# The first column tiles of an MLP's up projection by plain products on the mixer's own hi/lo parts, with the row squares read back from DRAM

## Chip, cores and metric

The kernel runs on one core of one Trainium2 chip. The metric is the device time of one execution in microseconds (us); shorter is better. All tensors are fp32. TensorE (PE) multiplies fp32 by splitting each operand into a high part and a low part and adding three passes (high by high, high by low, low by high), so one logical product costs three matmuls.

## The reference, cut to what matters

One decoder step for 512 prompt rows and 8 sample rows: a pooling mixer, an MLP, an attention layer, a second MLP. The change touches the end of the mixer and both MLPs.

```python
def _rmsnorm(x, g):
    y = x * lax.rsqrt(jnp.mean(x * x, axis=-1, keepdims=True) + RMS_EPS)
    return y * g
def _mlp_block(x, g, w_up, w_down):
    h = jnp.square(jax.nn.relu(_rmsnorm(x, g) @ w_up))
    return x + h @ w_down
# layer 0: x = x + pool_mix(rmsnorm(x, norm_mix[0])); x = _mlp_block(x, norm_mlp[0], ...)
# layer 1: x = x + attention(rmsnorm(x, ...)) @ w_o;  x = _mlp_block(x, norm_mlp[1], ...)
```

D_MODEL is 1024, D_FF 4096. Since relu and the square let a positive factor per row through, the kernel leaves out 1/rms(x) ahead of the up projection and multiplies the down projection's sum by its square, `rstd2`, near the end. So the squares of x are not needed when an MLP begins, only before its seventh block of columns is added up.

## The kernel before

**Layout.** The residual stream lies transposed in SBUF as `xT`: eight tiles (k = 0 to 7) of 128 features by 520 tokens, each token row cut in two halves of 260 (`HN`). A "product" (`product`, L186) is four k-tiles by three passes, 12 matmuls of 128x128 weights by 260 columns into half a PSUM bank. The tags `mm` and `aux` have four banks each.

**The up projection.** FF is cut into eight blocks `c` of 512 columns, each block into two pairs (`i` = 0, 1) of 128-column tiles. One pair is a 2 by 2 by 2 block product (two halves of k, two column tiles, two halves of tokens), which `up` computes by a Strassen-Winograd scheme: seven products instead of eight. For that it needs sums of weights (`fast_w`: VectorE makes four sums `wsum`, ScalarE and VectorE split seven operands into `whi` and `wlo`) and sums of inputs (`fast_x`: t1 to t4, made once per MLP from the scaled x, each split on ScalarE, L288, and VectorE, L289, into tiles named `first`, `xh` and `xl`). `fast_x` cannot begin before the rows of x that it reads are final. The relu output is squared and split (`squared`, L640 to L642) into `hh` and `hl`.

**The down projection.** `down(c)` makes 16 products per block and adds them into `xT` in place (for c = 0 it overwrites it; x itself was stored to a DRAM copy `xd` before and comes back as `xr` while c = 6 is added). Each block runs `up(c, 0)` and `up(c, 1)` interleaved with `down(c-1)` by a string of u and d; in every fifth place a `Steps` generator issues a piece of other work (compression of cached rows, with gathers `gat` on the GpSimd queue and their copies `perm`), after it has skipped its first eight calls.

**Squares.** `add_square` squares a tile of xT on ScalarE (L220, L223) and adds it on GpSimd (POOL, L225) into `sqacc`, through two buffers `sq`. The first MLP does this within its first two pairs; for the second MLP it is done in the loop that applies `w_o`, one square for each tile of xT. `mean_tok` and `spread` turn the sum into `rstd2` once the first pair of c = 1 is done.

**The mixer.** L161 multiplies eight k-tiles of pooled differences (`dh`, `dl`) by the mixer's weights and L604 adds the outcome to xT, on VectorE. Next to it four GpSimd operations (L556, L557, L608, L609) make the normalised rows `us` and `junk` that are stored as outputs, and the page numbers `idx` are made for the gathers.

**Order.** The program is not issued in the order in which it is written: a scheduler places the instructions of each engine by its own timeline, with the written order as priority. Each engine then works through its list strictly in order, and so a wait holds everything behind it. Weight loads (`wraw`, three buffers of 1 MB) go through SP's queue.

Of the kernel before, what the change touches and what calls it, by code (L numbers as in the profile page):

```python
# [9 lines left out]
F32 = mybir.dt.float32  # L10
# [8 lines left out]
P = 128  # L19
D = 1024  # L20
KT = D // P
# [81 lines left out]
def tile_step(ctx, tc, I, O):  # L103
# [6 lines left out]
    def pool(name, bufs=1, **kw):  # L110
        return tc.tile_pool(name=name, bufs=bufs, reuse_waits="tile", **kw)
# [162 lines left out]
    def fast_x(gcol, tp, first):  # L274
# [37 lines left out]
            split("t4", j, t4)  # L312
        return {n: [[t[:, k] for k in range(HK)] for t in hl] for n, hl in xs.items()}

    def part(tp):
        return tp.tile([P, 264], F32, name="part", tag="part", bufs=5)[:, :HN]

# [180 lines left out]
                self.skip = 0  # L498
                self()

    with pool("st") as st:
# [40 lines left out]
        for n, tiles in ((P, (0, 1)), (P, (2, 3)), (NB, (4,))):  # L542
            for i in tiles:
                t = xt[i] if i < 4 else xs
                junk = st.tile([P, D], F32, name="junk", tag="junk", bufs=2)
                S.activation(junk[:n], t, AF.Square, accum_out=ss[:n, i : i + 1])
            c = slice(tiles[0], tiles[-1] + 1)
            V.tensor_scalar(ss[:n, c], ss[:n, c], 1.0 / D, EPS, OP.mult, OP.add)
            rsqrt(rst[:n, c], ss[:n, c], rtmp[:n, c])
            for i in tiles:  # L550
                if i < 4:
                    bi = st.tile([P, 4, 144], F32, name=f"band{i}")
                    V.tensor_scalar(bi, band[:, min(i, 1)], rst[:, i : i + 1], None, OP.mult)
                    bands.append(bi)
                else:
                    G.tensor_scalar(us[:NB], xs, rst[:NB, 4:5], 1.0, OP.mult, OP.mult)  # L556
                    G.tensor_tensor(us[:NB], us[:NB], gbc[:NB], OP.mult)  # L557

        psx = bank()
        for k in range(KT):  # L560
# [11 lines left out]
                V.tensor_copy(dst, b.rearrange("p (k c) -> p k c", k=4))  # L572


        dh = st.tile([P, KT, TOK], F32R, name="dh")
        dl = st.tile([P, KT, TOK], F32R, name="dl")
# [31 lines left out]
        G.tensor_scalar(u3[96:128], xt[3][96:128], rst[96:128, 3:4], 1.0, OP.mult, OP.mult)  # L608
        G.tensor_tensor(u3[96:128], u3[96:128], gbc[96:128], OP.mult)  # L609
        nc.gpsimd.dma_start(O["pool_prompt"].rearrange("b a j d -> (b a j) d"), u3[113:128, :])  # L610
        nc.gpsimd.dma_start(O["pool_sample"][:, 0, 14, :], us[:NB])
        later.append(lambda: nc.sync.dma_start(O["pool_sample"][:, 0, 0:14, :], I["state_pool"][:, 0, 1:15, :]))
# [8 lines left out]
            V.tensor_tensor(idx[:, c], idf[:, c], pgf[:, 1:17], OP.add)  # L621


    def mlp(layer, gcol, mp, first, sqacc=None, filler=None, finish=None):


        xd = dram.tile([P, KT, TOK], F32, name=f"xd{layer}")
# [4 lines left out]
        steps = Steps(filler(mp) if filler else None, 8)  # L632
        nc_ = FF // (HK * P)
        hs = {}

# [9 lines left out]
        def up(c, i):  # L645
# [46 lines left out]
            for p in (p1, p5, p2, p6, p7, p3, p4) if c else (p1, p5, p6, p2, p7, p3, p4):  # L692
                p()
                yield

        def down(c):

            h = [[t[q] for t in hs[c]] for q in range(2)]
            for m in range(KT):
# [5 lines left out]
                for n in range(2):  # L705
# [6 lines left out]
                        V.tensor_tensor(y[:, hn], o, y[:, hn], OP.add)  # L712
                    if n and c == nc_ - 2:
                        x = mp.tile([P, TOK], F32, name="xr", tag="sq", bufs=2)
                        nc.scalar.dma_start(x, xd[:, m])
                        V.tensor_tensor(y, y, rstd2, OP.mult)  # L716
                        G.tensor_tensor(y, y, x, OP.add)  # L717
                    if c == nc_ - 1:
# [5 lines left out]
                            add_square(mp, sqacc, m)  # L724
                    yield

        w0 = fast_w(load_w(lambda r: [(r, wu[0])]), mp)
        xs = fast_x(gcol, mp, first)

        us_ = [up(0, i) for i in range(2)]  # L730
        for n, s_ in enumerate("00101001010111"):
            next(us_[int(s_)])
            if n == 3 and sqacc is None:
                sqacc = [mp.tile([P, TOK], F32, name="sqacc", tag="rs", bufs=1)]
                for k in range(KT):
                    add_square(mp, sqacc, k)
        for c in range(1, nc_):
            d = down(c - 1)
            for i in range(2):
                u = up(c, i)  # L740
# [4 lines left out]
                if c == 1 and i == 0:  # L745
# [20 lines left out]
        )  # L766
    with pool("mlp0") as mp:
        first = [[mp.tile([P, HK, HN], F32R, name=f"first{i}{j}") for j in range(2)] for i in range(3)]
        mean1 = mlp(0, gT[:, 16:24], mp, first, filler=compress_samples)


    with ExitStack() as at_:
# [490 lines left out]
        op_ = mp  # L1263
        sqacc = [op_.tile([P, TOK], F32, name="sqacc", tag="rs", bufs=1)]
# [78 lines left out]
    mlp(1, gT[:, 24:32], mp, first, sqacc, finish=finish)  # L1343
    mlp_.close()
    kx_.close()

# [36 lines left out]
```

## Time and profile before

| | before |
|---|---|
| median of 3 runs | 1203.05 us (1200.61 to 1206.67) |
| profiled execution | 1198.37 us, its span 1196.0 us |
| mean granted PE clock | 0.979 of full speed |
| PE busy | 1138.9 us, 95% of the span |
| DVE / ACT / POOL busy | 881.4 (74%) / 605.3 (51%) / 273.8 (23%) us |

The profile counts an engine busy while an instruction runs; PE's matmuls overlap, so its count of matmuls in a stretch says more than its busy time. The span is what the profiler sees between the first and the last instruction; the 2.4 us beside it are start and end. PE waits little over the whole span, but unevenly: of 40 equal slices the first three are its weakest.

### The profile page before, as it was taken

How to read it: one execution, taken by the hardware profiler on the slowest of the kernel's cores; microseconds unless marked ns; L12 is line 12 of the kernel's file. 1: busy time of each engine (PE TensorE's matmuls, PEld its weight loads, DVE VectorE, ACT ScalarE, POOL GpSimd, SP SyncE). 2: the span in 40 equal slices, each digit the busy share in tenths (PEclk: the TensorE clock that was granted, in tenths of full speed). 3: DMA queues.
4: the chain of work that ended last, by engine and by line, in shares of the span. 5: the costliest groups of instructions: out<-in, count | busy, mean ns of one | idle time of the engine just before them, and what ended most of it. 6: DMA issues, size and time to landing. Idle time of an engine off the chain costs nothing.

```text
span 1196.0 us, 22945 instructions
## 1 busy us (share of the span) xinstructions
PE 1138.9 (95%) x8971; PEld 1061.2 (89%) x8971; DVE 881.4 (74%) x2064; ACT 605.3 (51%) x1340; POOL 273.8 (23%) x311
## 2 busy tenths in 40 slices
PE   5769999999999999999998999999999999999996
PEld 4759999999999989999975665799999999999996
DVE  6888667777767887477678786769866686776885
ACT  4546544454444444554455555745654443544455
POOL 4350000011001323351458643712000000000032
PEclk9769999999999999999999999999999999999998
DMA  9424432343233426353321311143323323233221
GB/s 262 159 79 159 159 106 89 115 126 105 89 115 120 146 80 219 115 148 95 90 53 54 125 54 54 36 129 120 107 89 106 107 73 119 93 104 108 90 71 72
DMA packets 93539, 129.84 MB, mean 109 GB/s; under 512 B 5848, under 2 KB 68944, under 8 KB 92527
## 3 DMA queue, kind: packets, MB, share of 16 engines
q1 hardware_dynamic: 85687, 109.81, 29.4%
q0 software_dynamic: 5120, 14.23, 3.9%
q10 hardware_dynamic: 2624, 4.34, 1.3%
q8 instruction: 70, 1.15, 0.4%
q14 instruction: 38, 0.31, 0.1%
HBM read 115.76 MB, written 17.24 MB: 111 GB/s over the span
## 4 chain that ended last, share of the span: by engine, by line
PE 86%; DVE 6%; DMA 3%; ACT 2%; issue 1%; POOL 1%; SPq 0%; DVEq 0%; ACTq 0%; POOLq 0%
PE aux L191 29%; PE mm L191 27%; PE mm L161 14%; PE aux L1177 3%; PE aux L1204 3%; PE mm L1130 2%; PE aux L405 2%; DMA wraw<-in_w_up_dram 1%; DVE s L1135 1%; DMA wraw<-in_pool_w_dram 1%; POOL sqacc L225 1%; PE aux L236 1%; PE aux L449 1%; DVE wlo L149 1%; DVE wlo L183 1%
## 5 line engine op out<-in xcount | busy, mean ns | idle before, releaser
L191 PE MATMUL aux<-hh,whi 128*128 128x260 f32 x960 | 269.6, 283 | 1.5 <-DVE xT L712 1.5
L191 PE MATMUL aux<-hl,whi 128*128 128x260 f32 x960 | 269.6, 283 | 1.3 <-DVE hl L642 1.3
L191 PE MATMUL aux<-hh,wlo 128*128 128x260 f32 x960 | 266.3, 282 | 0.0
L182 ACT ACTIVATE whi<-wraw 128x512 fp32r<-128x512 f32 x224 | 132.3, 624 | 200.5 <-PE mm L191 155.0
L183 DVE TENSOR_TENSOR wlo<-wraw,whi 128x512 fp32r<-128x512 f32 x224 | 151.7, 701 | 56.1 <-ACT whi L182 51.5
L191 PEld LDWEIGHTS aux<-hl,whi 128*128 128x128 f32 x960 | 180.8, 188 | 1.9 <-DVE hl L642 1.5
L191 PEld LDWEIGHTS aux<-hh,whi 128*128 128x128 f32 x960 | 180.1, 188 | 2.7 <-DVE xT L712 1.2
L191 PEld LDWEIGHTS aux<-hh,wlo 128*128 128x128 f32 x960 | 179.0, 188 | 0.1
L191 PE MATMUL mm<-first,whi 128*128 128x260 f32 x768 | 152.1, 291 | 13.3 <-DVE first L289 8.7
L191 PE MATMUL mm<-xh,wlo 128*128 128x260 f32 x496 | 140.7, 285 | 0.0
L191 PE MATMUL mm<-xl,whi 128*128 128x260 f32 x496 | 140.6, 284 | 0.0
L191 PE MATMUL mm<-xh,whi 128*128 128x260 f32 x496 | 140.5, 284 | 0.0
L191 PEld LDWEIGHTS mm<-first,whi 128*128 128x128 f32 x768 | 124.3, 195 | 15.8 <-DVE first L289 10.2
L712 DVE TENSOR_TENSOR xT<-aux,xT 128x260 f32<-128x260 f32 x192 | 81.5, 424 | 49.0 <-PE aux L191 48.6
L191 PE MATMUL mm<-first,wlo 128*128 128x260 f32 x384 | 111.5, 291 | 3.7 <-DVE wlo L183 3.7
L717 POOL TENSOR_TENSOR xT<-xT,xr 128x520 f32<-128x520 f32 x16 | 24.7, 1546 | 371.1 <-DVE xT L716 371.1
L161 PE MATMUL mm<-xh,whi 128*128 128x260 f32 (+1 forms) x464 | 101.3, 287 | 1.4 <-DVE csm L1141 1.0
L161 PE MATMUL mm<-xl,whi 128*128 128x260 f32 (+1 forms) x464 | 101.9, 287 | 0.0
L161 PE MATMUL mm<-xh,wlo 128*128 128x260 f32 (+1 forms) x464 | 100.9, 286 | 0.0
L183 DVE TENSOR_TENSOR wlo<-wsum,whi 128x512 fp32r<-128x512 f32 x128 | 86.6, 688 | 16.2 <-ACT whi L182 15.6
L182 ACT ACTIVATE whi<-wsum 128x512 fp32r<-128x512 f32 x128 | 77.1, 623 | 38.0 <-PE mm L191 30.3
L191 PEld LDWEIGHTS mm<-xl,whi 128*128 128x128 f32 x496 | 94.1, 190 | 0.4
(329 smaller groups left out, 2527.3 us busy)
## 6 DMA issues: line engine op xcount, KB each, us to landing
wraw<-in_w_up_dram SPq DMA_DIRECT2D x32, 1024.0 KB, 5.9
wraw<-in_w_down_dram SPq DMA_DIRECT2D x32, 1024.0 KB, 5.2
wraw<-in_w_kv_dram SPq DMA_DIRECT2D x6, 1024.0 KB
xd<-xT SPq DMA_DIRECT2D x4, 1040.0 KB, 4.4
xr<-xd ACTq DMA_DIRECT2D x16, 260.0 KB, 3.6
w<-in_cmp_w_dram POOLq DMA_DIRECT2D x32, 128.0 KB, 3.2
wraw<-in_w_qg_dram SPq DMA_DIRECT2D x8, 512.0 KB, 5.6
wraw<-in_w_o_dram SPq DMA_DIRECT2D x16, 256.0 KB, 5.4
```

What stands on the lines that cost most here:

```text
L149: (eng or V).tensor_tensor(l_, raw_ap, f(h_), OP.subtract)
L161: T.matmul(o[n][:m, :HN], w[:, kt, :m], x[:, n * HN : (n + 1) * HN], start=(i == 0 and pi == 0), stop=(i == len(kts) - 1 and pi == 2),)
L182: S.activation(hi, raw_ap, AF.Copy)
L183: V.tensor_tensor(lo, raw_ap, f(hi), OP.subtract)
L191: T.matmul(o, w_[:, kt], x_[kt][:, xs], start=(start and kt == 0 and pi == 0), stop=(kt == HK - 1 and pi == 2), skip_group_check=True,)
L225: G.tensor_tensor(sqacc[0], sqacc[0], t, OP.add)
L405: T.matmul(acc[kv], w_[:, kv, b2], o_[:, b2 : b2 + 512], start=(t == 0 and i == 0 and b2 == 0), stop=(t == 7 and i == 2 and b2 == 1),)
L712: V.tensor_tensor(y[:, hn], o, y[:, hn], OP.add)
L717: G.tensor_tensor(y, y, x, OP.add)
L1130: T.matmul(b[:, : k1 - k0], qs[r][:, qt * P : (qt + 1) * P], ks[br][i][:, k0:k1], start=(i == 0), stop=(i == 1),)
L1177: T.matmul(o[par * HD : (par + 1) * HD], lhsT(par), pTs[par], start=start, stop=stop, skip_group_check=True,)
L1204: T.transpose(b[:, r * P : (r + 1) * P], sts[par][r][:, kt * P : (kt + 1) * P], ident)
```

## The change

1. The first MLP's first three pairs, (c, i) = (0,0), (0,1) and (1,0), go through a new `up_plain`: eight products per pair on x's own parts `xht`, `xlt`, with no sums of inputs or weights. These parts are made inside the mixer's loop (L648, L649 of the kernel after), and the weights of the first pair are loaded and split ahead of the mixer's loop.
2. `fast_t` takes the place of `fast_x` in the first MLP: `early()` makes t1 to t3 and an unsplit t4 while the first pairs run, and `last()` splits t4 into the places of b12 once the third pair no longer reads them.
3. In both MLPs the squares are taken from `xd`: a DMA on the GpSimd queue loads a tile into a `sq` buffer, ScalarE squares it in place, POOL adds it. `square` is called twice per pair in c = 1 and 2, and the mean is made in c = 3. The squares in the `w_o` loop go.
4. The `xr` loads move from ScalarE's queue to GpSimd's.
5. The rows `us` and `junk` are made by two VectorE instructions in place of four on GpSimd; `dh` and `dl` get a pool of their own; the filler skips three calls instead of eight.

```diff
+    def fast_t(gcol, tp, xht, xlt, ts):
...
+        def early():
+            for j in range(HK):
+                a, b = [tp.tile([P, TOK], F32, name="sq", tag="sq", bufs=2) for _ in range(2)]
+                for t, k in ((a, j), (b, j + HK)):
+                    S.activation(t, xT[k], AF.Copy, scale=gcol[:, k : k + 1])
+                t1, t2, t3 = [part(tp) for _ in range(3)]
+                t4 = hold[j // 2][:, j % 2 * HN : (j % 2 + 1) * HN]
+                V.tensor_tensor(t1, a[:, HN:], a[:, :HN], OP.subtract)
+                split("t1", j, t1)
+                V.tensor_tensor(t2, b[:, HN:], t1, OP.subtract)
+                split("t2", j, t2)
+                V.tensor_tensor(t3, b[:, HN:], a[:, HN:], OP.subtract)
+                split("t3", j, t3)
+                V.tensor_tensor(t4, b[:, :HN], t2, OP.subtract)
+
+        def last():
+            for j in range(HK):
+                split("t4", j, hold[j // 2][:, j % 2 * HN : (j % 2 + 1) * HN])
...
-                    G.tensor_scalar(us[:NB], xs, rst[:NB, 4:5], 1.0, OP.mult, OP.mult)
-                    G.tensor_tensor(us[:NB], us[:NB], gbc[:NB], OP.mult)
+                    V.scalar_tensor_tensor(us[:NB], xs, rst[:NB, 4:5], gbc[:NB], OP.mult, OP.mult)
...
+        raw0 = load_w(lambda r: [(r, I["w_up"][0][:, :256].rearrange("(k p) m -> p k m", p=P))])
+        plain0 = [split_q(raw0[:, q * HK : (q + 1) * HK, m * P : (m + 1) * P]) for m in range(2) for q in range(2)]
+        xht, xlt = new_x()
...
+                g_ = gT[:, 16 + k : 17 + k]
+                S.activation(xht[:, k], xT[k], AF.Copy, scale=g_)
+                V.scalar_tensor_tensor(xlt[:, k], xT[k], g_, f(xht[:, k]), OP.mult, OP.subtract)
...
+        def up_plain(c, i):
+
+            if c == i == 0:
+                w = plain[0]
+            else:
+                raw = load_w(lambda r: [(r, wu[c * 2 + i])])
+                w = [split_q(raw[:, q * HK : (q + 1) * HK, m * P : (m + 1) * P]) for m in range(2) for q in range(2)]
+            o = [[bank("mm")[:, :HN] for _ in range(2)] for _ in range(2)]
+            for q in range(2):
+                for m in range(2):
+                    for n in range(2):
+                        product(o[m][n], w[m * 2 + q], xs[f"b{q + 1}{n + 1}"], start=q == 0)
...
-                        nc.scalar.dma_start(x, xd[:, m])
+                        nc.gpsimd.dma_start(x, xd[:, m])
...
+        def square(k):
+            t = mp.tile([P, TOK], F32, name="sq", tag="sq", bufs=2)
+            nc.gpsimd.dma_start(t, xd[:, k])
+            if k in (0, KT - 1):
+                a = mp.tile([P, TOK], F32, name="sqacc", tag="rs", bufs=1) if k == 0 else t
+                S.activation(a, t, AF.Square)
+                sqacc.append(a)
+            else:
+                S.activation(t, t, AF.Square)
+                G.tensor_tensor(sqacc[0], sqacc[0], t, OP.add)
...
-                for q, s_ in enumerate("uuududdudududdd"):
+                for q, s_ in enumerate("uuuududdudududdd" if first_one else "uuududdudududdd"):
...
+                    if c < 3 and q in (3, 10):
+                        square((c - 1) * 4 + i * 2 + q // 10)
...
-                add_square(op_, sqacc, m)
```

Behind the last matmuls of the mixer (L161), PE's list before goes on with the products of two Winograd pairs in turn, on `first` tiles that `fast_x` makes:

```order
120 L161 MATMUL mm<-dl,whi 128x260
121 L161 MATMUL mm<-dh,wlo 128x260
122 L191 MATMUL mm<-first_446,whi 128x260
123 L191 MATMUL mm<-first_447,whi 128x260
124 L191 MATMUL mm<-first_446,wlo 128x260
125 L191 MATMUL mm<-first_446,whi 128x260
126 L191 MATMUL mm<-first_448,whi 128x260
127 L191 MATMUL mm<-first_447,whi 128x260
```

At the same place of the kernel after the products read `xh` and `xl`, the parts that the mixer's loop has written:

```order
116 L161 MATMUL mm<-dl,whi 128x260
117 L161 MATMUL mm<-dh,wlo 128x260
118 L191 MATMUL mm<-xh,whi 128x260
119 L191 MATMUL mm<-xl,whi 128x260
120 L191 MATMUL mm<-xh,wlo 128x260
121 L191 MATMUL mm<-xh,whi 128x260
122 L191 MATMUL mm<-xl,whi 128x260
```

What moved: the sums of inputs no longer stand between the mixer and PE's next work.

In the first MLP, POOL's list after holds a chain of loads and adds, where each load but the first three waits for an earlier add (names: `sq` is the loaded tile, `xd_486` the DRAM copy of x, `sqacc` the sum):

```order
24 L810 DMA sq<-xd_486 128x520 [waits DMAHW7_49,DVE_49,Activation_49]
25 L810 DMA sq<-xd_486 128x520 [waits DVE_49,Activation_49]
26 L810 DMA sq<-xd_486 128x520 [waits DMASW4_49,DMASW2_49,Activation_49]
27 L817 ISA
28 L817 TENSOR_TENSOR sqacc<-sqacc,sq 128x520 [waits Activation_49]
29 L810 DMA sq<-xd_486 128x520 [waits DMASW5_49,Pool_49]
30 L817 TENSOR_TENSOR sqacc<-sqacc,sq 128x520 [waits Activation_49]
```

Before, only adds stood there, each behind a square that ScalarE takes of xT itself.

ScalarE's list in the kernel after, at the start of the second MLP's products (`part` are copies of PSUM that the Winograd sums need, `whi` weight parts); the three squares shown are the fifth to seventh of this MLP, the eighth is the row behind them, followed by a `hh` and two `whi`, and the first four stand further up, in the `w_o` loop:

```order
727 L816 ACTIVATE sq<-sq 128x520 [waits DMASW3_49,Pool_49]
728 L698 ACTIVATE part<-mm 128x260 [waits DVE_49,PE_49]
729 L816 ACTIVATE sq<-sq 128x520 [waits DMASW4_49,Pool_49]
730 L182 ACTIVATE whi<-wraw 128x512 [waits PE_49]
731 L182 ACTIVATE whi<-wsum 128x512
732 L698 ACTIVATE part<-mm 128x260 [waits DVE_49,PE_49]
733 L698 ACTIVATE part<-mm 128x260 [waits DVE_49]
734 L182 ACTIVATE whi<-wsum 128x512 [waits PE_49]
735 L182 ACTIVATE whi<-wraw 128x512
736 L698 ACTIVATE part<-mm 128x260 [waits DVE_49,PE_49]
737 L728 ACTIVATE relu<-relu 128x520 [waits DVE_49]
738 L816 ACTIVATE sq<-sq 128x520 [waits DMASW5_49,Pool_49]
```

Before, the last square stands in front of those copies and waits for xT on VectorE and for POOL:

```order
745 L223 ACTIVATE sq<-xT 128x520 [waits DVE_49,Pool_49]
746 L283 ACTIVATE xg<-xT,gT 128x520
747 L182 ACTIVATE whi<-wsum 128x512 [waits PE_49]
748 L182 ACTIVATE whi<-wsum 128x512
749 L288 ACTIVATE xh<-part 128x260 [waits DVE_49]
```

What moved: although `square` is written in c = 1 and 2, the scheduler has put all eight squares of the second MLP at its very start, and four of them now stand among the copies and splits of the first pairs, behind loads from DRAM.

## Rows read from the trace of the kernel before

**Rows 1.** Windows: length, each engine's busy time (instructions), granted PE clock, DMA share, GB/s.

```profile
36.00:48.00 12.00, 11.93 (x99) 11.72 (x99) 7.75 (x18) 3.20 (x6) 0.00 (x0) 1.00 0.22 90
48.00:60.00 12.00, 5.41 (x18) 4.21 (x18) 12.00 (x21) 12.00 (x29) 9.39 (x10) 0.58 0.53 177
60.00:75.00 15.00, 8.38 (x34) 7.11 (x33) 15.00 (x32) 7.18 (x19) 10.15 (x6) 0.54 0.46 157
75.00:85.00 10.00, 6.14 (x32) 5.84 (x33) 6.96 (x17) 3.54 (x10) 6.04 (x2) 0.66 0.00 0
85.00:90.00 5.00, 5.00 (x44) 5.00 (x43) 4.46 (x9) 3.92 (x10) 0.00 (x0) 1.00 0.05 12
900.00:1000.00 100.00, 100.00 (x836) 100.00 (x835) 70.02 (x134) 43.82 (x87) 0.00 (x0) 1.00 0.33 106
```

**Rows 2.** Waits from 48 to 85 us: engine, line, releaser, total, times, longest.

```profile
POOL gat L373 <- PE mm L161: 17.1, 1, 17.1
ACT sq L223 <- POOL sqacc L225: 9.0, 1, 9.0
PE mm L191 <- DVE first L289: 8.7, 5, 4.2
```

**Rows 3.** Groups of VectorE's and ScalarE's instructions from 48 to 85 us.

```profile
L183 DVE TENSOR_TENSOR wlo<-wraw,whi 128x512 fp32r<-128x512 f32 x3 | 2.1, 684 | 0.9 <-ACT whi L182 0.9
L223 ACT ACTIVATE sq<-xT 128x520 f32<-128x520 f32 x7 | 4.1, 622 | 9.0 <-POOL sqacc L225 9.0
```

**Rows 4.** VectorE's residual adds within the mixer, 36 to 48 us.

```profile
L604 DVE SCALAR_TENSOR_TENSOR xT<-mm,gT,xT 128x260 f32<-128x260 f32 x16 | 7.8, 489 | 3.8 <-PE mm L161 3.6
```

**Rows 5.** POOL's timeline behind the mixer: start, length, instructions, idle before.

```profile
48.09 1.05 POOL L373 DMA_INDIRECT gat<-in_cache_kv_pages_dram,idx  x1 [17.08 <-PE mm L161]
...
50.84 3.00 POOL L359 DMA_DIRECT2D w<-in_cmp_w_dram  x4
53.84 2.78 POOL L225 TENSOR_TENSOR sqacc<-sqacc,sq 128x520 f32<-128x520 f32 x2
...
70.54 10.58 POOL L225 TENSOR_TENSOR sqacc<-sqacc,sq 128x520 f32<-128x520 f32 x2
```

**Rows 6.** DMA issues of the whole span: queue, count, size, median us to landing.

```profile
xd<-xT SPq DMA_DIRECT2D x4, 1040.0 KB, 4.4
xr<-xd ACTq DMA_DIRECT2D x16, 260.0 KB, 3.6
w<-in_cmp_w_dram POOLq DMA_DIRECT2D x32, 128.0 KB, 3.2
```

**Rows 7.** Windows at the start of the second MLP, columns as in group 1.

```profile
825.00:830.00 5.00, 4.81 (x38) 4.39 (x36) 5.00 (x15) 5.00 (x15) 0.00 (x0) 1.00 0.87 279
830.00:835.00 5.00, 4.15 (x32) 3.94 (x33) 5.00 (x14) 3.36 (x11) 0.00 (x0) 1.00 0.39 147
835.00:840.00 5.00, 4.41 (x34) 4.00 (x34) 3.12 (x6) 2.81 (x7) 0.00 (x0) 1.00 0.00 0
840.00:850.00 10.00, 10.00 (x86) 10.00 (x85) 10.00 (x19) 7.87 (x17) 0.00 (x0) 1.00 0.36 107
```

**Rows 8.** One of POOL's adds in the `w_o` loop.

```profile
815.26 3.45 POOL L225 TENSOR_TENSOR sqacc<-sqacc,sq 128x520 f32<-128x520 f32 x1 [3.46 <-ACT sq L223]
```

**Rows 9.** SP's queue: the store of x's second half, start of the second MLP.

```profile
824.83 0.34 SPq L629 DMA_DIRECT2D xd<-xT  x1
```

**Rows 10.** ScalarE's timeline there: `part` copies, then a wait.

```profile
831.83 0.64 ACT L654 ACTIVATE part<-mm 128x260 f32<-128x260 f32 x2
...
837.20 0.63 ACT L182 ACTIVATE whi<-wraw 128x512 fp32r<-128x512 f32 x1 [3.83 <-PE mm L191]
```

**Rows 11.** PE's waits from 395 to 450 us, around the end of the first MLP.

```profile
PE aux L191 <- DVE xT L712: 1.5, 2, 1.0
PE aux L405 <- DVE ol L401: 1.3, 1, 1.3
```

**Rows 12.** PE's longest wait in the attention stage, 600 to 800 us.

```profile
PE mm L1130 <- DVE pmx L1135: 3.7, 4, 2.1
```

More of the change, by code (lines that the diff above doesn't have):

```diff
@@ L313, in fast_x, with split @@
         return {n: [[t[:, k] for k in range(HK)] for t in hl] for n, hl in xs.items()}
+    def fast_t(gcol, tp, xht, xlt, ts):
+        parts = {}
+        for q in range(2):
+            for n in range(2):
+                v = [t[:, q * HK : (q + 1) * HK, n * HN : (n + 1) * HN] for t in (xht, xlt)]
+                parts[f"b{q + 1}{n + 1}"] = v
+        xs = {n: parts[n] for n in ("b11", "b12", "b21", "b22")}
+        xs.update({f"t{i + 1}": t for i, t in enumerate(ts)})
+        xs["t4"] = parts["b12"]
+        def split(n, j, v):
+            h, l = xs[n][0][:, j], xs[n][1][:, j]
+            S.activation(h, v, AF.Copy)
+            V.tensor_tensor(l, v, f(h), OP.subtract)
+        hold = [tp.tile([P, TOK], F32, name="t4", tag="hh", bufs=8) for _ in range(2)]
+        def early():
[15 more added lines that the diff above has]
+                split("t4", j, hold[j // 2][:, j % 2 * HN : (j % 2 + 1) * HN])
+        return {n: [[t[:, k] for k in range(HK)] for t in hl] for n, hl in xs.items()}, early, last
     def part(tp):
@@ L499, in rest @@
                 self()
-    with pool("st") as st:
+    with pool("st") as st, pool("sd", side="right") as sd:
         xt = []
@@ L572, in tile_step @@
                 V.tensor_copy(dst, b.rearrange("p (k c) -> p k c", k=4))
-        dh = st.tile([P, KT, TOK], F32R, name="dh")
-        dl = st.tile([P, KT, TOK], F32R, name="dl")
+        dh = sd.tile([P, KT, TOK], F32R, name="dh")
+        dl = sd.tile([P, KT, TOK], F32R, name="dl")
         pws = [split_w(pw[:, :, m * P : (m + 1) * P], eng=V) for m in range(2)]
@@ L621, in tile_step, with mlp @@
             V.tensor_tensor(idx[:, c], idf[:, c], pgf[:, 1:17], OP.add)
-    def mlp(layer, gcol, mp, first, sqacc=None, filler=None, finish=None):
+    def mlp(layer, gcol, mp, first, filler=None, finish=None, plain=None):
         xd = dram.tile([P, KT, TOK], F32, name=f"xd{layer}")
@@ L631, in mlp @@
         wd = I["w_down"][layer].rearrange("(c k p) (j m) -> c j p k m", p=P, k=HK, m=512)
-        steps = Steps(filler(mp) if filler else None, 8)
+        steps = Steps(filler(mp) if filler else None, 3)
         nc_ = FF // (HK * P)
@@ L694, in up @@
                 yield
+        def up_plain(c, i):
[5 more added lines that the diff above has]
+            o = [[bank("mm")[:, :HN] for _ in range(2)] for _ in range(2)]
+            for q in range(2):
+                for m in range(2):
+                    for n in range(2):
+                        product(o[m][n], w[m * 2 + q], xs[f"b{q + 1}{n + 1}"], start=q == 0)
+                        if q and n == 0:
+                            r = mp.tile([P, TOK], F32, name="relu", tag="relu", bufs=2)
+                        if q:
+                            S.activation(r[:, n * HN : (n + 1) * HN], o[m][n], AF.Relu)
+                        if q and n:
+                            hs.setdefault(c, []).append(squared(r))
+                        yield
         def down(c):
@@ L725, in down @@
                     yield
[L727 to L736, printed above, removed]
+        if plain:
+            xs, early, last = fast_t(gcol, mp, plain[1], plain[2], first)
+            for i in range(2):
+                for _ in up_plain(0, i):
+                    pass
+            early()
+        else:
+            w0 = fast_w(load_w(lambda r: [(r, wu[0])]), mp)
+            xs = fast_x(gcol, mp, first)
+            us_ = [up(0, i) for i in range(2)]
+            for s_ in "00101001010111":
+                next(us_[int(s_)])
+        sqacc = []
+        def square(k):
[5 more added lines that the diff above has]
+                sqacc.append(a)
+            else:
+                S.activation(t, t, AF.Square)
+                G.tensor_tensor(sqacc[0], sqacc[0], t, OP.add)
         for c in range(1, nc_):
@@ L739, in mlp @@
             for i in range(2):
-                u = up(c, i)
-                for q, s_ in enumerate("uuududdudududdd"):
+                first_one = plain and c == 1 and i == 0
+                if first_one:
+                    quarter()
+                u = (up_plain if first_one else up)(c, i)
+                for q, s_ in enumerate("uuuududdudududdd" if first_one else "uuududdudududdd"):
                     next(u if s_ == "u" else d)
@@ L744, in mlp @@
                         steps()
-                if c == 1 and i == 0:
+                    if c < 3 and q in (3, 10):
+                        square((c - 1) * 4 + i * 2 + q // 10)
+                if first_one:
+                    last()
+                if c == 3 and i == 0:
                     mean = mean_tok(sqacc)
@@ L768, in tile_step @@
         first = [[mp.tile([P, HK, HN], F32R, name=f"first{i}{j}") for j in range(2)] for i in range(3)]
-        mean1 = mlp(0, gT[:, 16:24], mp, first, filler=compress_samples)
+        mean1 = mlp(0, gT[:, 16:24], mp, first, filler=compress_samples, plain=(plain0, xht, xlt))
     with ExitStack() as at_:
@@ L1341, in finish @@
         nc.sync.dma_start(O["y_sample"].rearrange("b t d -> (b t) d"), ys)
-    mlp(1, gT[:, 24:32], mp, first, sqacc, finish=finish)
+    mlp(1, gT[:, 24:32], mp, first, finish=finish)
     mlp_.close()
```

5 lines of the change are left out of this document (1 added, 4 removed).

## The prediction

> **What bounds the kernel now.** The windows come first, because the share of the whole span (PE busy 95%) hides one bad stretch. In full flow PE issues 836 matmuls in 100 us, so one costs 0.12 us and a product of 12 costs 1.44 us [rows 1]. The mixer runs at that rate and at full clock up to 48 us. Then, from 48 to 85 us, PE issues only 18 + 34 + 32 = 84 matmuls, which at full rate are 10.1 us of work, in 37 us; the granted clock there is 0.54 to 0.66, with 1.2 GHz the lower of its two levels. From 85 us on the rate and the clock are full again. So about **26.9 us** are lost in one place, behind the mixer.
>
> The waits name who is late there: PE's longest wait is for VectorE's `first`, the low parts of the input sums, 8.7 us in five pieces [rows 2]. VectorE is busy for all 27 us from 48 to 75 [rows 1], ScalarE for all of the first 12. Later ScalarE is held 9.0 us by POOL's square sums [rows 2], two adds that took 10.58 us at 70.54, where two at 53.84 took 2.78 [rows 5]. What the reader is to see: the sums of x, of weights, the splits and the squares are all asked for at once when the mixer ends, and PE has nothing else. The rest of the loss of time is the slow clock, which follows the gaps.
>
> **The change part by part.**
>
> *Removed: the starvation, -26.9 us.* Three pairs now need only `xht`, `xlt` and split weights. The first pair's weights are split before the mixer ends, and PE's list goes from the mixer's last matmul straight to `xh`. If PE never waits behind the mixer, the 37 us shrink to the 10.1 us of their matmuls.
>
> *Added: matmuls, +4.3 us.* Eight products instead of seven in three pairs are 3 x 12 = 36 matmuls at 0.12 us, at full clock.
>
> *The mixer's loop, 0 (-1 to +2.7).* VectorE's 16 adds take 7.8 us [rows 4] of the mixer's 12. Eight `xl` come to it; no row shows a 128x520 operation of that form, the nearest is a 128x512 split at 684 ns [rows 3], so 5.5 us, in all 13.3 us against PE's 12. The 1.3 us too many are covered: the first pair's first four products read k = 0 to 3 only, and so the last four `xl` have 4 x 1.44 = 5.8 us. If that cover went, PE would wait these 1.3 us. The four weight splits that move ahead are 4 x 0.684 = 2.7 us of VectorE, the upper bound; below nothing lies what the four GpSimd operations gave up to VectorE, at most 1 us by estimate.
>
> *Between the first pairs, +1 (0 to 3).* The second pair needs PSUM banks back from the first, and the relu that frees them stands in ScalarE's list behind `w1h`, a split that waits for a load on POOL's queue. POOL still starts its gathers at the mixer's end [rows 2, 5], its loads are out at 53.8 and land 3.2 us later [rows 6], at 57; the second pair begins at 48 + 8 x 1.44 = 59.5. That fits by 2.5 us, less the instructions between. I take 1; a load that lands twice as late gives 3.
>
> *`early`, 0.* Its 4 x 8 VectorE operations of 128x260, at most 0.49 us each [rows 4], are 15.7 us, beside 12 more splits of 0.68 us, 8.2 us [rows 3]; PE's three pairs and the first of `down(0)` are 24 products and more, over 35 us. They cover it.
>
> *Squares of the first MLP, +1.5 (0 to 4).* One of the two `sq` buffers goes round in: issue 0.75 us (four took 3.00) [rows 5], landing 3.6 us (the `xr` loads, of the same size, on ScalarE's queue) [rows 6], square 0.62 us [rows 3], add 1.39 to 3.45 us [rows 5, 8]. That is 6.4 to 8.4 us, so with two buffers a square each 3.2 to 4.2 us. By the order PE has some 28 matmuls between two squares in this stage, 3.4 us. So ScalarE is held by 0 to 0.8 us per square, at most some 6 us over seven; it is half idle, and PE sees the rest of it late. I take 1.5.
>
> *Squares of the second MLP, +4 (0 to 10).* Here the order puts all eight at the very start. The first four stand in the `w_o` loop. The fifth needs x's second half in DRAM: its store is issued at 824.83 [rows 9] and lands 4.4 us later, then the load's 0.75 + 3.6: about 833.6. ScalarE comes to it at about 831.8, where its `part` copies now stand [rows 10], and these wait behind. The seventh and eighth need an add and a load more: 833.6 + 0.6 + 1.4 to 3.4 + 4.35 = 840 to 842, and one more link for the last, 843 to 846; behind it a `hh` and two weight splits wait, which PE asks for at about 843. ScalarE has a free wait of 3.83 us between the two places [rows 10], which takes up part. Two stalls of 2 us each make the 4; nothing if the slack takes all, 10 if both links are as long as the longest add.
>
> *Squares gone from the `w_o` loop, -1 (-1.6 to 0).* From 825 to 840 PE is idle 0.19 + 0.85 + 0.59 = 1.6 us [rows 7] with VectorE full, behind a loop where POOL's adds take up to 3.45 us [rows 8]. *Filler five calls earlier, -1 (-2.8 to 0):* PE's waits at the end of the first MLP are 2.8 us [rows 11]. *`xr` on POOL's queue, 0:* issue, landing and add are about 6 us for a buffer, 3 us per tile with two; PE takes 30 products for eight tiles, 5.4 us each, and covers it. *Order elsewhere, 0 (-3.7 to +3.7):* the scheduler shuffles the attention stage too, whose longest wait totals 3.7 us [rows 12].
>
> **Sum.** -26.9 + 4.3 + 0 + 1 + 1.5 + 4 - 1 - 1 = -18.1 us. The profiled execution was 1198.37 us (span 1196.0 and 2.4 beside it), so it goes to 1180.3. It lies 4.7 us under the median of the runs; taken off that, 1203.05 - 18.1 gives **1185 us**.
>
> One rule of the Trainium skill speaks against the squares' chain: its page "SBUF — State Buffer" (section "Who interferes with whom") says that a VectorE instruction with two SBUF inputs and a GpSimd instruction that reads SBUF exclude each other, the later one blocking for the whole of the other. The two adds of 10.58 us agree with it; the two of 2.78 us, also with VectorE busy throughout, do not show it. With 5.3 us for each add the sum would be that of rival 2.
>
> **The rivals.**
>
> 1. *The squares cost nothing in PE's time.* ScalarE is only half busy and itself waits for PE [rows 10]. Then the sum is -18.1 - 1.5 - 4 = -23.6, with no stall between pairs -24.6: **1178 to 1179 us**. Against it: four squares stand directly ahead of what PE needs.
>
> 2. *The squares' chain sets the pace; slower than before.* If each add beside a busy VectorE takes 5.3 us, as at 70.54 [rows 5], a buffer goes round in 0.75 + 3.6 + 0.62 + 5.3 = 10.3 us, a square each 5.1 us, and ScalarE is held 7 x (5.1 - 3.4) = 12 us in each MLP. If it all reaches PE that is 24 us, which eats the 23.6, and a lower clock behind the gaps makes it slower: **1203 to 1210 us**. The point is 1.5 us of PE's time per square, 16 times. Against it: VectorE was full in the windows of the 2.78 us pair too [rows 1, 5].
>
> 3. *The gap moves.* PE runs dry behind the first pair, because `w1h` or the second pair's splits come late, and the clock drops again, as it did at 48. Gaps of 3 us, and 10 us of work at some 0.6 of the clock, cost about 8 to 10 us: **1193 to 1195 us**. For it: the load margin is 2.5 us. Against it: three loads of weights are ahead, and VectorE has lost the Winograd sums at this place.
>
> 4. *The change doesn't fill PE*, as PE waits for `xl` where it waited for `first`. Eight `xl` at 0.684 us cannot hold it longer than about 5 us beyond the mixer; with a slow clock behind, 1192. It counts with rival 3.
>
> **Chances.** The forecast 0.5, its own range 1180 to 1192. Rival 1 0.22, rivals 3 and 4 together 0.20, rival 2 0.08. The range from 1176 to 1198 holds rival 1 and 3, and the bounds of single terms (all good ends together give 1175, all bad ones 1204). A measurement of this kernel tells a change from none at about 0.5%, 6 us. Faster, under 1197: the forecast, rival 1 and most of 3 and 4, **0.87**. Within 0.5%: **0.07**. Slower: most of rival 2, **0.06**.
>
> **What would show it.** PE's windows from 48 to 85 at over 40 matmuls per 5 us with clock 1.00, and the wait for `first` gone, show the first term; under 30 in any of them is rival 3. 36 more matmuls in the page. In ScalarE's waits, lines L813 and L816 for DMA: a total of under 10 us in each MLP is the forecast, over 12 with PE waits for `part`, `whi` or `hh` behind them is rival 2. At the second MLP's start PE's idle time should rise from 1.6 us to some 5. Wrong it would be made most by a stall that I have no row for: loads on POOL's queue of 260 KB, which no run has shown, and the new order of the attention stage.

## The result and the profile after

| | before | after | ratio (95% interval) |
|---|---|---|---|
| median | 1202.92 us (4 runs) | 1187.59 us (4 runs, 1185.42 to 1189.76) | 0.987 (0.9835 to 0.9905) |
| profiled execution | 1198.37 us, span 1196.0 | 1185.42 us, span 1183.6 | |
| PE matmuls, busy | 8971, 1138.9 us | 9007, 1138.5 us | |

The medians lie 15.3 us apart, the profiled executions 12.95 us. The forecast was 18.1 us less, 1185 us.

The windows of after, with the columns of [rows 1], at the place where the kernel before starved:

```profile
48.00:60.00 12.00, 8.12 (x68) 7.92 (x66) 3.24 (x7) 3.09 (x8) 5.97 (x6) 0.97 0.89 305
60.00:75.00 15.00, 13.68 (x96) 13.68 (x97) 10.66 (x21) 7.14 (x17) 3.83 (x4) 0.80 0.20 56
75.00:85.00 10.00, 10.00 (x86) 10.00 (x85) 9.00 (x18) 7.93 (x17) 0.00 (x0) 1.00 0.64 220
```

From 48 to 85 us PE now issues 68 + 96 + 86 = 250 matmuls, against 84 [rows 1]. (Added up over windows, a matmul on an edge counts twice; one window from 48 to 85 counts 247 and 82.) Full flow would be 309, so 59 matmuls, **7.1 us**, are still missing, all between 56 and 70 us. The wait for `first` is gone, and another has come. The waits of after from 48 to 90 us (engine, line, releaser, total, times, longest):

```profile
DVE perm L423 <- DMA gat<-in_cache_kv_pages_dram,idx: 8.8, 1, 8.8
...
PE mm L191 <- DVE xl L649: 5.2, 1, 5.2
```

And VectorE's timeline there (start, length, instruction, idle before):

```profile
59.84 0.76 DVE L423 COPY perm<-gat 128x512 f32<-128x512 f32 x2 [8.76 <-DMA gat<-in_cache_kv_pages_dram,idx]
60.51 0.76 DVE L649 SCALAR_TENSOR_TENSOR xl<-xT,gT,xh 128x520 fp32r<-128x520 f32 x1
```

The reader is to see the order of these two rows: the last `xl`, which the first plain pair needs, stands behind two copies of gathered rows (one row, x2), and those wait 8.8 us for a gather, while VectorE does nothing; the `xl` ahead of them had started at 50.32 us. (The high and low parts are the kernel's own work, made on ScalarE and VectorE, and the three passes of a product are three matmuls that it issues; so a late `xl` stops PE.) The gathers were issued at the mixer's end; the second one in POOL's timeline:

```profile
48.40 2.87 POOL L412 DMA_INDIRECT gat<-in_cache_kv_pages_dram,idx  x1 [0.30 <-issue]
```

Its instruction ended at 51.27 us and its rows were used at 59.84. From 48 to 60 us the DMA engines were 0.89 busy, against 0.53 before [rows 1]; SP issued the next weight load at 50.10 us, where before it came at 61.03. That this load made the gather late is likely, but no run shows it.

A second loss lies where nothing was changed. One window from the attention stage's first `kvt` (VectorE's scaling of a tile of its keys and values) to the first score matmul, in before and in after:

```profile
475.03:586.65 111.62, 111.14 (x934) 108.64 (x935) 69.22 (x124) 51.42 (x87) 43.99 (x46) 1.00 0.43 119
```

```profile
456.49:575.43 118.94, 114.49 (x935) 111.39 (x935) 69.43 (x123) 51.45 (x87) 43.79 (x45) 0.97 0.39 109
```

The same instructions take 7.3 us longer. The waits of PE in after, 500 to 600 us, say "issue", which means that the engine waited for nothing that the profile shows:

```profile
PE mm L161 <- issue: 4.0, 5, 1.7
```

So by stages: at the first `kvt` after is 475.03 - 456.49 = 18.5 us ahead; it loses 7.3 in this pause, and gains another 1.2 in all that comes behind (the rest of the attention stage, the `w_o` loop and the second MLP), which makes the 12.4 us between the spans. The second MLP's start, where squares were feared, in before and after (25 us each, from about the last residual add on):

```profile
825.00:850.00 25.00, 23.38 (x186) 22.34 (x185) 23.12 (x50) 19.03 (x48) 0.00 (x0) 1.00 0.39 128
```

```profile
812.60:837.60 25.00, 22.34 (x177) 21.31 (x176) 21.80 (x47) 19.75 (x48) 7.63 (x7) 1.00 0.50 170
```

Nine matmuls fewer, 1.1 us; PE's idle time is 2.7 us in place of 1.6.

### The profile page after: what moved, and what is told of

Read it like the earlier page. It is cut to its first block, busy times and chain, and to the rows that moved or that the text cites. A ratio compares the mean times of both kernels' runs of the same rounds, so it can differ in the third digit from the quotient of the medians.

```text
span 1183.6 us, 22979 instructions
## 1 busy us (share of the span) xinstructions
PE 1138.5 (96%) x9007; PEld 1062.8 (90%) x9007; DVE 858.7 (73%) x2032; ACT 598.8 (51%) x1321; POOL 275.8 (23%) x339
## 4 chain that ended last, share of the span: by engine, by line
PE 79%; DVE 7%; DMA 5%; issue 4%; POOL 2%; ACT 1%; SPq 0%; DVEq 0%; POOLq 0%; ACTq 0%
PE aux L191 26%; PE mm L191 26%; PE mm L161 11%; PE aux L1266 3%; PE mm L1219 3%; PE aux L1293 3%; PE aux L444 2%; DMA sq<-xd 1%; DMA gat<-in_cache_kv_pages_dram,idx 1%; DVE wlo L183 1%; DMA xd<-xT 1%; DMA wraw<-in_w_up_dram 1%; DMA w<-in_cmp_w_dram 1%; PE aux L488 1%; PE mm L629 1%
## 5 line engine op out<-in xcount | busy, mean ns | idle before, releaser
L191 PE MATMUL mm<-xl,whi 128*128 128x260 f32 x552 | 157.2, 285 | 5.2 <-DVE xl L649 5.2
L191 PE MATMUL mm<-xh,wlo 128*128 128x260 f32 x552 | 156.7, 285 | 0.2 <-DVE wlo L183 0.2
L191 PE MATMUL mm<-xh,whi 128*128 128x260 f32 x552 | 155.9, 284 | 0.0
L191 PE MATMUL mm<-first,whi 128*128 128x260 f32 x696 | 132.8, 285 | 0.3 <-ACT relu L733 0.3
L191 PEld LDWEIGHTS mm<-first,whi 128*128 128x128 f32 x696 | 109.6, 190 | 1.0 <-ACT relu L733 0.5
L191 PEld LDWEIGHTS mm<-xl,whi 128*128 128x128 f32 x552 | 105.0, 190 | 5.7 <-DVE xl L649 5.4
L161 PE MATMUL mm<-xh,whi 128*128 128x260 f32 (+1 forms) x464 | 102.2, 289 | 3.4 <-issue 2.0
L191 PEld LDWEIGHTS mm<-xh,wlo 128*128 128x128 f32 x552 | 104.9, 190 | 0.6 <-DVE wlo L183 0.4
L191 PEld LDWEIGHTS mm<-xh,whi 128*128 128x128 f32 x552 | 104.6, 190 | 0.4
L161 PE MATMUL mm<-xl,whi 128*128 128x260 f32 (+1 forms) x464 | 102.2, 288 | 1.3 <-issue 1.3
L161 PE MATMUL mm<-xh,wlo 128*128 128x260 f32 (+1 forms) x464 | 101.4, 287 | 0.7 <-issue 0.7
L191 PE MATMUL mm<-first,wlo 128*128 128x260 f32 x348 | 99.6, 286 | 0.6 <-DVE wlo L183 0.6
L182 ACT ACTIVATE whi<-wsum 128x512 fp32r<-128x512 f32 x116 | 69.6, 623 | 40.4 <-PE mm L191 29.8
```

The source lines that it names most:

```text
L161: T.matmul(o[n][:m, :HN], w[:, kt, :m], x[:, n * HN : (n + 1) * HN], start=(i == 0 and pi == 0), stop=(i == len(kts) - 1 and pi == 2),)
L182: S.activation(hi, raw_ap, AF.Copy)
L191: T.matmul(o, w_[:, kt], x_[kt][:, xs], start=(start and kt == 0 and pi == 0), stop=(kt == HK - 1 and pi == 2), skip_group_check=True,)
```

## The experiments

The runs came in three groups, each on one chip with the kernel before beside it; the first and the third were on the same chip, the second on another. The kernel before took 1196.23, 1202.66 and 1200.11 us in the three groups, so times are compared within a group, and ratios across.

**The change again, and its parts (first group).** `after_again` is the changed kernel, unedited.

> The changed kernel once more. Theory: the pause of some 5.8 us around 560 to 577 us of the profiled execution, where PE waited for nothing that the profile shows, belongs to that one execution; then the profile has no such stretch, the wait of about 5 us for L649's xl stays, and the time is 1184 to 1191 us. Rival: the pause comes from the new order of the attention stage; then it is there again, at the same place and of about the same length.

1181.18 us (1177.6 to 1182.5), ratio 0.9874 (0.9848 to 0.9899): the result stands. (The time lies under the expected range, and so does the next one's, as the kernel before is 6.7 us faster here, too.) The pause is not there:

```profile
458.02:569.67 111.65, 111.17 (x935) 108.66 (x935) 69.22 (x123) 51.43 (x87) 43.45 (x45) 1.00 0.42 116
```

The wait for `xl` is there, 5.2 us again. From 48 to 85 us PE issues 72 + 87 + 86 = 245 matmuls, 7.7 us short of full flow.

`late_gather` keeps everything, but queues the first gathered rows' copies and weight split behind `early()`:

```diff
             early()
+            for e_ in (mybir.EngineType.DVE, mybir.EngineType.Activation):
+                marks.append(next(i_ for i_ in reversed(nc.cur_bb.bb.instructions) if i_.engine == e_))
...
+            with ExitStack() as behind:
+                for i_ in marks if t == 0 else []:
+                    behind.enter_context(tc.issue_after(i_))
```

> The copies perm of the first gathered rows, and the split w1h, stand behind the last instructions of early() on their engines. Theory: PE's wait of 5.2 us for xl came only from the copies ahead of the last xl on VectorE, which waited for the gather; with the matmuls at half clock behind it it cost 7 us, so 1180 us (1177 to 1183), and 48 to 75 us runs at over 40 matmuls per 5 us. Rival: what the filler has done early must now be done later, and the gain comes back as waits at the end of the first MLP or in the attention stage: 1184 to 1188 us.

1173.46 us (1172.85 to 1174.66), ratio 0.9817 (0.9798 to 0.9836), 7.7 us faster than `after_again`, just what the missing 64 matmuls of that trace cost. Its windows have no gap and the clock never falls:

```profile
48.00:60.00 12.00, 12.00 (x102) 12.00 (x101) 9.31 (x20) 8.81 (x21) 6.42 (x6) 1.00 0.89 306
60.00:75.00 15.00, 15.00 (x128) 15.00 (x127) 9.96 (x18) 7.38 (x16) 0.00 (x0) 1.00 0.32 107
75.00:85.00 10.00, 10.00 (x85) 10.00 (x85) 9.71 (x27) 9.37 (x25) 2.22 (x3) 1.00 0.56 180
```

The DMA engines are as busy as in after (0.89); the gather may land late, since nobody on PE's path stands behind it. The rival, that the delayed filler gives it back later, falls. The edit moves the copies and the split `w1h` together; the trace of after has no wait of ScalarE for `w1h` in this stretch, so the copies were the cause.

`wo_squares` takes the second MLP's squares in the `w_o` loop again:

```diff
                     V.tensor_tensor(xs_, o[n][:, :HN], xs_, OP.add)
+                add_square(mp, sqacc, m)
...
-                    if c < 3 and q in (3, 10):
+                    if not sqs and c < 3 and q in (3, 10):
```

> The second MLP's squares again in the w_o loop, from xT, as before; all else as after. The prediction's terms (4 us for the chain from DRAM, 1 us given back by the w_o loop) say about 3 us faster than the kernel after, 1184 to 1185 us. The trace of after says that the start of the second MLP lost only about 0.7 us against before: then within 1 us of the kernel after.

1177.37 us (1175.65 to 1180.44), ratio 0.9844 (0.9824 to 0.9864), 3.8 us below `after_again`, with runs that overlap. Of this 2.4 us stand in the two traces already at the first `kvt` (458.02 against 455.58), ahead of any square of the second MLP, so it was not settled; it comes again below.

`squares_only` is the kernel before with the squares of both MLPs from DRAM and nothing else:

```diff
-            if n == 3 and sqacc is None:
-                sqacc = [mp.tile([P, TOK], F32, name="sqacc", tag="rs", bufs=1)]
-                for k in range(KT):
-                    add_square(mp, sqacc, k)
...
+                    if c < 3 and q in (3, 10):
+                        square((c - 1) * 4 + i * 2 + q // 10)
```

> The kernel before with the squares from DRAM in both MLPs and nothing else. Theory: what starves PE behind the mixer are the input sums on VectorE, and the 9 us for which POOL held ScalarE lie partly beside them: 3 to 6 us faster than before, 1197 to 1200 us. Rival: the squares made the starvation; then most of the gain is here, 1188 to 1192 us. A third: its squares take the place of input splits on ScalarE right behind the mixer, and it is slower than before.

1197.13 us (1193.33 to 1202.32, 10 runs), ratio 1.0014 (0.9993 to 1.0036): no change. My 3 to 6 us fell, and so did the rival that the squares made the starvation; the third was right that they come among the input splits, but the time is no longer. The hold by POOL's adds is gone, but the scheduler puts the squares right behind the mixer here, and PE waits for ScalarE's `part` copies, which stand behind a square that waits for its load:

```profile
PE mm L191 <- ACT part L654: 15.5, 1, 15.5
ACT sq L744 <- DMA sq<-xd: 14.8, 3, 13.1
```

The load's issue was itself late, at 73.27 us, behind a gather on POOL's queue:

```profile
56.37 14.00 POOL L373 DMA_INDIRECT gat<-in_cache_kv_pages_dram,idx  x1 [1.73 <-DVE perm L384]
```

So the move of the squares brought nothing without the plain pairs. It doesn't show what the move is worth by itself: one hold took the place of another here, and without the long gather the time might have been another.

**How much cover do the sums need (second group)?** `late_two` and `late_one` are `late_gather` with two plain pairs and with one, and `late_xt_squares` is `late_gather` with the first MLP's squares taken of xT behind the mixer.

```diff
-                first_one = plain and c == 1 and i == 0
+                first_one = False
```

> Like late_gather, but the third pair, (1,0), goes by seven products again, so the input sums must be done within two plain pairs (23 us of PE) instead of three. Theory: VectorE has about 27 us of work there (sums and their splits 15 us, weight sums and splits of the third pair 8, squares 5), so PE runs dry for about 4 us and saves 12 matmuls, 1.4 us: 3 us slower than late_gather, 0.984 of before. Rival: two pairs are cover enough; then it is 1.4 us faster than late_gather, 0.980 to 0.981 of before.

1184.01 us, ratio 0.9833 (0.9802 to 0.9865). PE does run dry, and for longer than expected:

```profile
75.00:85.00 10.00, 6.62 (x39) 5.62 (x37) 9.30 (x28) 7.61 (x20) 1.11 (x2) 0.87 0.42 156
85.00:90.00 5.00, 3.35 (x15) 3.35 (x16) 3.17 (x5) 3.79 (x8) 4.44 (x5) 0.50 0.58 157
```

39 + 15 = 54 matmuls in 15 us where 125 fit: 8.5 us lost, for waits of only 5 us in sum; the rest is the clock at 0.50 behind them. Less the 1.4 us of saved matmuls that is 7, and the time is 7.5 to 9 us above the two kernels of this group with three plain pairs. The waits are 2.8 us for ScalarE's `first` and 1.7 for its `whi`, and only 0.5 for VectorE's low parts, so they name ScalarE as the last link, where the theory had VectorE alone.

```diff
-            for i in range(2):
-                for _ in up_plain(0, i):
-                    pass
+            for _ in up_plain(0, 0):
+                pass
             early()
+            last()
+            quarter()
+            for _ in up(0, 1):
+                pass
```

> Like late_gather, but only the first pair is plain; the second and third go by seven products, so the sums have 11.6 us of cover. Theory (PE starves for as long as VectorE is not done with the sums): PE runs dry for 10 to 15 us behind the first pair, partly at half clock, and saves 24 matmuls, 2.9 us: 9 to 14 us slower than late_gather, 0.989 to 0.994 of before. Rival (what mattered was the burst right behind the mixer alone): within 3 us of late_gather.

1186.69 us, ratio 0.9862 (0.9834 to 0.989), 10 to 12 us above those two: the difference that the theory gave. The ratio itself is below the expected one, but ratios move that much between groups: `late_gather` had 0.9817 in the first and 0.9782 in the third, on one chip. The gap stands at 60 to 80 us, right behind the one plain pair:

```profile
60.00:75.00 15.00, 8.91 (x48) 7.69 (x46) 12.96 (x33) 8.73 (x21) 1.11 (x2) 0.80 0.42 138
75.00:85.00 10.00, 9.73 (x65) 9.53 (x66) 9.20 (x13) 7.69 (x18) 5.00 (x6) 0.80 0.35 88
```

That is 113 matmuls in 25 us where 209 fit, 11.5 us. So it is not the burst behind the mixer alone; each pair of cover taken away shows as a gap.

```diff
+            sqacc = [mp.tile([P, TOK], F32, name="sqacc", tag="rs", bufs=1)]
+            for k in range(KT - 1):
+                add_square(mp, sqacc, k)
             early()
```

> Like late_gather, but the first MLP's squares are taken of xT right behind the mixer as before, all eight added on POOL, while the plain pairs run; the eighth goes into the same sum. Theory: in this place ScalarE's relus and splits queue behind squares that wait for POOL's adds, and VectorE is full, so PE runs dry for 3 to 8 us: 0.984 to 0.989 of before. Rival: the plain pairs leave ScalarE time enough, and the move of the squares to DRAM bought nothing here: within 1 us of late_gather, 0.981 to 0.983.

1176.46 us, ratio 0.9776 (0.9747 to 0.9806): faster than either expectation, and 1.5 us from its neighbour in this group, `late_wo_squares`, with intervals that overlap. PE waits 1.1 us for a relu and no more, though POOL's adds are the same ones that held ScalarE 9 us before:

```profile
54.63 9.33 POOL L226 TENSOR_TENSOR sqacc<-sqacc,sq 128x520 f32<-128x520 f32 x6
```

Six adds in 9.33 us, 1.56 each. ScalarE still waited 4.2 us for one of them, so my theory, that its relus would queue behind the adds, was right in kind; in PE's time it came to 1.1 us and not to 3 to 8. VectorE paid as well: three of its two-input instructions beside the adds, at 57.50, 62.72 and 64.44 us, took 1.79 to 1.83 us, and the same forms 0.68 to 0.69 elsewhere in this trace.

> Like late_gather, with the second MLP's squares in the w_o loop as before. If those squares from DRAM cost what wo_squares showed against after_again (3.8 us between medians whose runs overlap), it is 3 to 4 us faster than late_gather, 0.978 to 0.979 of before. If that was scatter, as the stages of the two traces say, within 1.5 us of late_gather, 0.980 to 0.983.

1174.93 us, ratio 0.977 (0.9741 to 0.9798). Against `late_gather`'s 0.9817 of another group and chip that would be 5 us, and without `late_gather` in this group it could not be judged.

**The squares on one chip (third group).**

> The kernel before once more, for a profile on the chip of the next three. The changed kernels paused for some 7 us within L161's matmuls of the attention stage on one chip and not on another. Theory: the pause belongs to the chip, so the kernel before has it where the others of this call have it, and its stage from the first kvt to the first score matmul is as long as theirs. Rival: it belongs to the changed order, and the kernel before shows 111.6 us there whatever the others show.

One execution: 1196.24 us. No kernel of this group paused at the place in question, the kernel before neither, so the question that it was to answer stays open.

> late_gather once more, beside the next two on one chip: the yardstick for the place of the squares. 0.977 to 0.983 of before, as the two chips so far have given for its family.

1173.37 us (1172.1 to 1175.08), ratio 0.9782 (0.9759 to 0.9805).

> The second MLP's squares in the w_o loop, on the chip of late_gather_b. Theory from the stages of the traces: within 1.5 us of late_gather_b. Rival, the prediction's term of 3 us: 3 to 4 us faster than it.

1173.01 us (1169.33 to 1175.08), ratio 0.9771 (0.9744 to 0.9798): 0.4 us from its yardstick.

`late_no_dram` takes both MLPs' squares of xT (the edits of `late_xt_squares` and `wo_squares` together).

> No squares from DRAM at all: both MLPs take them of xT at the old places, with late_gather's order else. Theory: the first MLP's squares behind the mixer cost some 1 us (PE waited 1.1 us for relu in late_xt_squares), the second's nothing: within 2 us of late_gather_b. Rival: the loads from DRAM cost PE time in both MLPs, 1.5 and 4 us by the prediction's terms: 4 us or more faster than late_gather_b.

1171.57 us (1170.36 to 1175.74), ratio 0.9772 (0.9746 to 0.9799). All three intervals hold each other's ratio. Once the pairs are plain and the gather's copies are out of the way, the place of the squares makes no difference that can be told, in either MLP; the intervals would hide one of 2 to 3 us.

## Why the prediction came out as it did

1. **Starvation, -26.9.** Right in kind and place. PE's list went straight on, the wait for `first` went, and `late_gather` gives the whole term: 102 + 128 + 85 = 315 matmuls from 48 to 85 us, none missing (one on the edge of two windows counts in both). In the changed kernel itself 7.1 us of it are still lost, so the term measured -19.8.
2. **The mixer's loop, 0.** This is the step that failed. The price was right: VectorE's 16 adds took 7.3 us there and an `xl` 0.75, so eight take 6.0, in all 13.3. The cover was not: "the last four `xl` have 4 x 1.44 = 5.8 us" holds only if nothing that waits stands between them on VectorE. The two `perm` copies stood ahead of the last one, waited 8.8 us for the gather, and PE waited 5.2, with 2 us more at half clock. I gave the gather's landing no price and looked only at `w1h` on ScalarE.
3. **Between the first pairs, +1.** No wait there in after: the relu that I feared for waited itself 5.3 us for PE. Rival 4 named the wait that came, PE's for `xl`, and its size, 5 us and a slow clock behind; its reason was another, the length of the eight `xl`, and these were only 0.75 us each. The sign set for rival 3, under 30 matmuls in 5 us, did show (7 from 58 to 63 us), but that rival's gap behind the first pair did not come: PE stopped within the pair, for the wait of rival 4.
4. **Matmuls, +4.3.** 36 more in the page.
5. **Squares, +1.5 and +4, less 1 for the `w_o` loop.** Mis-sized: 0 in the first MLP (PE waits for nothing from 90 to 200 us), about 1 at the start of the second by the windows, and together under the scatter by `late_no_dram`. ScalarE's waits for the loads came to 0.7 us in the first MLP and 4.7 in the second. The terms let its slack take only a part of such waits; its wait of 3.83 us for PE [rows 10] may have been the cover, which no run shows by itself. POOL's adds took 1.32 to 1.83 us in the first MLP of after, where rival 2 needed 5.3. The rule on the shared port in the Trainium skill ("SBUF — State Buffer", "Who interferes with whom") agrees with the trace all the same, but on the other engine's side:

```profile
98.04 1.82 POOL L817 TENSOR_TENSOR sqacc<-sqacc,sq 128x520 f32<-128x520 f32 x1 [1.03 <-ACT sq L816]
98.60 1.80 DVE L183 TENSOR_TENSOR wlo<-wsum,whi 128x512 fp32r<-128x512 f32 x1
100.33 0.68 DVE L183 TENSOR_TENSOR wlo<-wraw,whi 128x512 fp32r<-128x512 f32 x1
```

   The split that came while an add ran took 1.80 us, the same form 0.68 just behind it. The prediction read the pair of adds of 2.78 us before [rows 5] as no sign of this; but beside it VectorE's instructions at 53.91 and 55.38 us took 1.55 and 1.78 us, where their forms took 0.42 and 0.68 nearby. Looking at the adds alone, I missed who paid.
6. **Filler earlier, -1.** At the first `kvt` after is 18.5 us ahead; points 1 and 4 make 26.9 - 7.1 - 4.3 = 15.5, and 3.0 are left. The traces show little of it to be the filler's. PE's last matmul of the mixer started at 46.48 us in after and at 47.65 in before, which is 1.2, and from run to run this moves by as much (46.92 in `after_again`). From 465 to 470 us the clock of before fell to 0.66 and PE issued 30 matmuls where some 42 fit, 1.4 us; there was no such fall in after, nor in `before_again`. PE's waits for the filler's `ol` fell from 3.0 to 2.3 us. No run had the filler alone.
7. **Order elsewhere, 0 (-3.7 to +3.7).** The pause of 7.3 us lies outside of that bound. It is in the trace of after and not in that of `after_again`, so it is no part of what the change does to the order. The bounds were also added up unevenly: "all bad ends together" hold this term's +3.7, "all good ones" leave out its -3.7 and would be 1171 us with it, not 1175.

The sum by the profiled executions: at the first `kvt` 18.5 us are gained where the terms up to there gave 21.1 (the gap takes 7.1, less 1 for point 3, 1.5 for the squares and 2 more under point 6); the pause takes 7.3; behind it 1.2 are gained where the terms gave a loss of 3. So 1185 us came near 1187.6 partly by luck: the gap that was not priced and the squares that were priced too high cancel in part. The pause is not needed for this account. Without it `after_again` was 15.05 us below the kernel before by medians, with it after was 15.3 below, and points 1 and 4 alone give 19.8 - 4.3 = 15.5. Stages far from the change scatter by some 3 us between executions: from the first score matmul to the first residual add of `w_o` the one kernel took 191 us in after and 194 in `after_again`, the other 193 in before and 190.5 in `before_again`.

What was shown: the gap's cause (`late_gather`), the need of three pairs of cover (`late_two`, `late_one`), that the place of the squares does not matter, to some 2 us, once PE is fed. Only argued: point 6. Parts 4 and 5 of the change were in no run alone; PE's waits for `xT` at the end of the first MLP, where `xr` is used, were 1.4 us in after and 1.5 in before.

## What to carry to other kernels

When a burst of preparation starves TensorE behind a stage, a plainer and longer form of the first products, on operands that the stage before can leave ready, may buy the time in which the preparation for the cheaper form is made: 4.3 us of extra matmuls bought back some 27. Then walk each engine's list from the stage's end and ask of every instruction ahead of the needed one what it waits for, transfers above all: two copies that waited for a gather cost 7.7 of the 22.8 us that `late_gather` gains, a third, and putting them behind the sums was the one edit here that clearly gained. Cost a held engine only by what is left of its slack. And where one of two engines looks unhurt by the other, look at how long the other's instructions took.

## What the runs showed of the hardware that was not expected

- **Who pays when GpSimd's adds meet VectorE's two-input instructions.** Beside an add that had begun, VectorE took some 1.8 us for what else took 0.68 (point 5). The other way round, in before the two adds of 10.58 us [rows 5] ended at 81.12 us, and VectorE had gone on with such instructions without a break from before their start at 70.54 until 78.62; then it was idle:

```profile
80.77 0.63 DVE L289 TENSOR_TENSOR xl<-part,xh 128x260 fp32r<-128x260 f32 x1 [2.15 <-ACT xh L288]
```

  From 78.62 to 81.12 are 2.5 us, about two adds of 1.3 us, the least that one took in after. That the adds waited for that break is read from the times; no run changed the order to test it.
- **A pause without a releaser.** In the profiles of after and of all four kernels of the second group, PE's L161 matmuls in the attention stage (L162 in the four) waited 3.4 to 4.0 us in five or six pieces for nothing that the profile shows, and the stage took about 119 us; in all eight profiles of the first and the third group, which were on one other chip, and in that of before, it took 111.6 to 111.7 us. `late_wo_squares` has it and its repeat `late_wo_squares_b` has not, and their ratios are 0.977 and 0.9771. So either the kernel before pauses on the second group's chip as well, where it took 1202.66 us and no profile of it was taken, or the time came back elsewhere. The cause is open.
- **A gather's instruction on GpSimd that takes 10 to 14 us.** It took 0.95 to 1.7 us in most places, 2.5 to 2.9 for the second gather behind the mixer in most kernels with the change (2.87 in after at 48.40), 10.44 in `late_xt_squares` and in `late_no_dram`, and 14.00 in `squares_only` at 56.37, there holding all that stood behind it on that queue. In the three long ones VectorE worked without a break, in `squares_only` until 69.48 us, 0.9 us before the gather's end; but it did so beside a gather of 1.23 us at 58.45 in before, too. The cause is open.
- **What a short wait costs.** In `late_two` 5 us of waits became 8.5 us of lost matmuls, as the granted clock went to 0.50 behind them.
